# First Fourier factor, direct S5 products and angle tables in another order, the tables in smaller pieces

## The chip, the cores and the metric

One core of a Trainium2 chip runs the whole kernel. The metric is the time of one execution on the device, in microseconds (us). Of several executions the median is given.

## What is computed

The kernel computes two layers of a trunk over 2048 latent tokens (a grid of width 64) and 256 context tokens, 1024 channels wide, in fp32. The first layer has two branches side by side: a Fourier mixer and a windowed attention. The second layer's branches are a gated MLP and a bidirectional linear recurrence (S5). Cut to the lines that matter:

```python
def even_mixer(hl, hc, w_in, ...):
    fa_l, ga_l, q_l, k_l, v_l, gb_l = split_cols(hl @ w_in, EVEN_SPLITS)
    a_l = fourier_mix(fa_l) * jax.nn.silu(ga_l)
    n_l = neighbourhood_attention(heads(q_l), heads(k_l), heads(v_l), k_c, v_c, rpb) * jax.nn.silu(gb_l)
    y_l = jnp.concatenate([a_l, n_l], axis=-1) @ w_out

def fourier_mix(v):
    y = jnp.fft.fftn(vg, axes=(1, 3), norm="ortho").real

def s5_discretise(lam_re, lam_im, log_step, b_re, b_im):
    dt = jnp.exp(log_step)[:, None]
    lam_bar = jnp.exp(lam * dt)
    b_bar = ((lam_bar - 1.0) / lam)[..., None] * lax.complex(b_re, b_im)

def s5_direction(u_lat, u_ctx, ...):
    h_lat = linear_scan(lam_bar, drive(u_lat), h_end, reverse)
    return read(h_lat)
```

The 2048-point transform over positions is done as two factors (16 times 128). The recurrence's tables depend on weights alone and are made during the first layer.

## The kernel before

The program of the first layer stands in `run`. The normalised input is kept on the chip as two fp16 halves, hh and hl, and a weight as wh and wl; an fp32 product is three fp16 passes into one PSUM tile pg (`mm3`, L181). In this order, the program does:

- `fourier_proj`: the Fourier branch's projection; its rows go to memory as fa_d.
- `s5_prep` (L1116): the recurrence's tables. It ends in two parts. The direct products (L1298 to L1330) load ws and bs from memory for each of eight q, multiply them (matmuls of L1319), mask and add on DVE (L1329) and store kp_d. The angle tables (L1332 to L1340) are complex products of two "turn" tables by `cmul` (L1109 to L1114, six DVE operations); each of eight pieces (four j, two directions d) is a tile rot of 128x2304, stored to rot_d by SP (L1340). The pool of the turn tables, s5r, lies on the left side of memory and is closed behind them.
- `v_proj` (L528): the values in three blocks of 256 columns, 18 tiles of 128 tokens each. Blocks 0 and 1 are called from within `s5_prep`, block 2 after it.
- `fourier_first` (L548): for each of 16 n2 it loads a factor d and the transposed rows Z of fa_d (L559, L561), multiplies (L564), copies on ScalarE (ACT) and stores A_d (L567); then come the context's part (L573, L577) and its output ys (L581). d and Z have three buffers each.
- `heads` (L686): for each of six pairs of heads the weights, then ten tiles of Q and K (drained into stg, stored as qd and kd, L739 and L741) and five gate tiles (drained into gate, L526). It is a generator of steps: `need((0, 5))` runs all steps of pair 0, and the attention takes the later ones as filler.
- `attention` (L817): the pool "units", on the right side. The loads (masks L883, K L911, Vc L917, G L920, Q L905, V L931) are issued on SP. For each unit a score tile S (L997, one buffer) is followed by the softmax on DVE (L1000, into P) and ACT (L1002), transposes PT (L1016), their split into halves, and the value product pv (L1030, L1033).

All loads and stores of this stretch go through SP's one queue, in program order. The compiler's scheduler decides each engine's order by its own estimates; inside the attention PE's order is that of the code, where `fill` puts QK and gate tiles of the coming pairs between scores. Every engine runs its own list in order, and a wait at its head holds all that follow.

Much later, in the second layer, the tables are read back as E (L1650): one piece (j, d) is read in two halves h, four runs of 1152 B for each partition and half.

Of the kernel before, what the change touches and what calls it, by code (L numbers as in the profile page):

```python
# [9 lines left out]
F32 = mybir.dt.float32  # L10
# [44 lines left out]
class Kern:  # L55
# [137 lines left out]
    def run(self):  # L193
        with ExitStack() as st:
# [13 lines left out]
            with self.pool_("ps0", space=PSUM) as self.ps:  # L208
# [4 lines left out]
                with self.pool_("gemm", side="right") as gp:  # L213
# [334 lines left out]
    def fourier_first(self, pool):  # L548
# [7 lines left out]
        self.gg_d = self.dram.tile([2, 128, SEQ], F32, name="gg_d")  # L556
        for n2 in range(16):
# [558 lines left out]
    def s5_prep(self, between):  # L1116
# [7 lines left out]
        self.rot_d = self.dram.tile([4, 2, 128, 2 * 4 * 288], F32, name="rot_d")  # L1124
        self.mag8 = self.const.tile([128, 32], F32, name="mag8")
        rots = ExitStack()
        rp = rots.enter_context(self.pool_("s5r"))

        turn = [rp.tile([128, 2, 32, n], F32, name=f"turn{n}") for n in (16, 18)]
# [166 lines left out]

        with self.stream(""):
            between[1]()  # L1298
        with self.pool_("s5pk") as pool:
# [571 lines left out]
```

## Time and profile before

| | before |
|---|---|
| median of 3 runs | 2426.11 us (2421.2 to 2430.19) |
| the profiled execution's own time | 2425.14 us |
| its span in the trace | 2423.3 us |
| mean granted clock of PE | 0.965 |
| PE busy | 2219.7 us (92%) |
| DVE busy | 1579.7 us (65%) |
| ACT busy | 1050.9 us (43%) |
| DMA, mean rate | 141 GB/s |

The span runs from the first to the last instruction of the trace; the 1.8 us by which the execution's own time is longer lie around it. Busy shares are averages over stages with different limits, so the stage in question is read by windows and timelines. A timeline row gives the start and duration of a group of like instructions, and in brackets the idle time before it and what ended it. [...]

### The profile page before, as it was taken

Reading aid. Unit: us, or ns where it says so; the run is one execution under the profiler, and the core shown is the slowest. Engines: PE = TensorE matmul, PEld = TensorE weight load, DVE = VectorE, ACT = ScalarE, POOL = GpSimd, SP = SyncE. Lnnn points to the kernel's source line nnn. Section 1 sums busy time; section 2 is a strip of 40 time slices with the busy share of each in tenths; the row PEclk is TensorE's granted clock in tenths of the full one; section 3 lists DMA queues with packets and bytes.
Section 4 is the critical chain, followed back from the end, with each engine's and each line's share of the span. In section 5 each row is a group of like instructions: output and inputs, shape, how many; then the busy total and the mean of one; then the engine's idle time right before and its main releaser. Section 6 shows DMA issues by size and latency. Waiting matters only on the chain. (4 is left out here: it accounts for less than half of the span.)

```text
span 2423.3 us, 42852 instructions
## 1 busy us (share of the span) xinstructions
PE 2219.7 (92%) x15860; PEld 1421.6 (59%) x15860; DVE 1579.7 (65%) x3949; ACT 1050.9 (43%) x2212; POOL 336.3 (14%) x457
## 2 busy tenths in 40 slices
PE   5999885999999999999978899997899999999998
PEld 2668773476665767666657466556555565444443
DVE  5888892266567666666569667774496952458455
ACT  4822222155555656565557454552221221334332
POOL 0102200022222322222234000000010011110000
PEclk8999998999999999999998899998899999999999
DMA  9844677413335243433342444545466751256332
GB/s 320 264 108 127 168 236 231 131 54 95 115 103 149 81 119 106 116 114 93 96 167 86 137 140 135 158 134 164 143 182 195 200 152 48 80 156 194 122 113 87
DMA packets 349971, 340.57 MB, mean 141 GB/s; under 512 B 94482, under 2 KB 291486, under 8 KB 347970
## 3 DMA queue, kind: packets, MB, share of 16 engines
q1 hardware_dynamic: 349650, 337.80, 46.5%
q8 instruction: 125, 2.05, 0.4%
q14 instruction: 84, 0.69, 0.1%
q10 hardware_dynamic: 112, 0.03, 0.0%
HBM read 218.43 MB, written 110.91 MB: 136 GB/s over the span
## 5 line engine op out<-in xcount | busy, mean ns | idle before, releaser
L181 PEld LDWEIGHTS <-wh 128*128 128x128 f16 x2944 | 281.8, 99 | 169.0 <-issue 9.2
L1000 DVE CUSTOM_DVE_ANT_0 P<-S,bias,slab 128x640 f32<-128x640 f32 (+2 forms) x216 | 193.6, 896 | 161.0 <-PE S L997 157.0
L189 ACT ACTIVATE ph<-PT 128x384 f16<-128x384 f32 (+1 forms) x408 | 172.6, 456 | 216.4 <-PE PT L1016 215.6
L181 PEld LDWEIGHTS <-wl 128*128 128x128 f16 x1472 | 144.0, 100 | 112.0 <-issue 27.4
L190 DVE SCALAR_TENSOR_TENSOR pl<-PT,ph 128x384 f16<-128x384 f32 (+1 forms) x408 | 195.0, 508 | 13.8 <-ACT ph L189 12.4
L949 POOL TENSOR_TENSOR bias<-G,masks 128x384 f32<-128x384 f32 (+1 forms) x144 | 152.3, 1058 | 345.5 <-DVE t L1000 322.5
L1002 ACT ACTIVATE P<-P,t 128x640 f32<-128x640 f32 (+2 forms) x216 | 181.2, 839 | 41.4 <-DVE t L1000 40.0
L181 PE MATMUL pg<-hh,wl 128*128 128x512 f16 (+1 forms) x800 | 184.6, 365 | 13.7 <-DVE stg L190 5.6
L181 PEld LDWEIGHTS <-h1p 128*128 128x128 f16 x1152 | 111.1, 98 | 136.6 <-issue 8.8
L181 PE MATMUL pu<-wh,h1p 128*128 128x512 f16 x768 | 179.9, 379 | 1.6 <-DMA h1p<-h 1.6
L181 PE MATMUL pg<-hl,wh 128*128 128x512 f16 (+1 forms) x800 | 181.2, 360 | 0.0
L181 PE MATMUL pg<-hh,wh 128*128 128x512 f16 (+1 forms) x800 | 181.2, 359 | 0.0
L181 PEld LDWEIGHTS <-yh 128*128 128x128 f16 x1088 | 106.8, 98 | 125.4 <-issue 2.7
L1016 PE MATMUL PT<-ident,P 128*128 128x128 f32 x1104 | 162.3, 277 | 11.3 <-DVE pl L190 9.8
L997 PEld LDWEIGHTS <-Q 128*128 128x128 f16 x1776 | 131.6, 98 | 63.1 <-issue 22.7
L997 PE MATMUL S<-K,Q 128*128 128x128 f16 (+1 forms) x1776 | 158.4, 233 | 2.4 <-DVE t L1000 2.2
L181 PE MATMUL pg<-wh,yl 128*128 128x512 f16 x544 | 133.3, 386 | 5.2 <-DVE yl L190 5.1
L1016 PEld LDWEIGHTS PT<-ident,P 128*128 128x128 f32 x1104 | 120.3, 142 | 20.2 <-issue 6.8
L181 PE MATMUL pg<-wl,yh 128*128 128x512 f16 x544 | 131.3, 382 | 0.0
L156 DVE TENSOR_REDUCE t<-wf 128x1 f32<-128x1024 f32 x68 | 82.4, 1216 | 74.8 <-DMA wf<-in_w_in_even_dram 27.0
L181 PE MATMUL pg<-wh,yh 128*128 128x512 f16 x544 | 130.3, 379 | 0.0
L181 PEld LDWEIGHTS <-hh 128*128 128x128 f16 x1152 | 115.5, 100 | 15.7
(344 smaller groups left out, 3952.6 us busy)
## 6 DMA issues: line engine op xcount, KB each, us to landing
wada<-in_w_ada_dram SPq DMA_DIRECT2D x34, 512.0 KB
x<-in_x_dram SPq DMA_DIRECT2D x32, 512.0 KB
wf<-in_w_in_even_dram SPq DMA_DIRECT2D x28, 512.0 KB
V<-vs SPq DMA_DIRECT2D x192, 64.0 KB
K<-kd SPq DMA_DIRECT2D x96, 128.0 KB
wf<-in_w_in_odd_dram SPq DMA_DIRECT2D x20, 512.0 KB
rot_d<-rot SPq DMA_DIRECT2D x8, 1152.0 KB
Y<-ys SPq DMA_DIRECT2D x144, 64.0 KB
```

What stands on the lines that cost most here:

```text
L156: nc.vector.tensor_reduce(m[:, i:i + 1], f, axis=AX.X, op=OP.max, apply_absolute_value=True)
L181: nc.tensor.matmul(ps, a(k), b(k), start=(n == 0), stop=(n == 3 * kb - 1))
L189: nc.scalar.activation(hi, src, AF.Copy, scale=scale)
L190: nc.vector.scalar_tensor_tensor(lo, src, scale, hi, op0=OP.mult, op1=OP.subtract)
L949: nc.gpsimd.tensor_tensor(q4(bv), gv, q4(masks[:, m0:m0 + 128 * nch]), op=OP.add)
L997: nc.tensor.matmul(S[:, at:at + m], u["q"], K[:, hl, off:off + m], start=(hl == 1), stop=(hl == 0))
L1000: nc.vector.tensor_tensor_reduce(P[:, 0:n], S[:, 0:n], u["B"][:, 0:n], u["negf"], 3.4e38, OP.add, OP.min, nm)
L1002: nc.scalar.activation(P[:, 0:n], P[:, 0:n], AF.Exp, bias=nm, scale=-1.0, accum_out=l)
L1016: self.nc.tensor.transpose(PT[:, c - a:c - a + 128], P[:, c:c + 128], self.ident)
```

## The change

`s5_prep` is cut into three. Its first part, with value blocks 0 and 1, stays where it is. The direct products become `s5_direct`, which loads ws and bs for two j at a time and no longer for four. The angle tables become `s5_angles`: sixteen pieces of half the size, in the layout in which E is read back. The turn tables' pool goes to the right side of memory and stays open to the end.

`fourier_first` becomes a generator that issues its first four pairs of loads and then yields. The new order of the program is: tables of S5, value blocks 0 and 1; weights of pair 0; the Fourier factor's first loads; value block 2; the rest of the Fourier factor; the direct products; all steps of pair 0; the angle tables, in a pool of their own on the right side; the attention.

```diff
-                    with self.stream("b"):
-                        self.s5_prep([lambda: self.v_proj(gp, 0), lambda: self.v_proj(gp, 1)])
-                    self.v_proj(gp, 2)
-                    qp = hTs.enter_context(self.pool_("qkg"))
-                    with self.pool_("fft") as fp, self.stream("f"):
-                        self.fourier_first(fp)
-                    self.gpool = hTs.enter_context(self.pool_("gates"))
-                    self.steps = self.mixed(self.heads(qp), self.ada_steps(), ADA_EVERY)
-                    self.ahead, self.credit, self.at, self.made = None, 0.0, (0, 0), -1
-                    self.need((0, 5))
+                    with self.pool_("s5r", side="right") as rp:
+                        with self.stream("b"):
+                            self.s5_prep(rp, [lambda: self.v_proj(gp, 0), lambda: self.v_proj(gp, 1)])
+                        qp = hTs.enter_context(self.pool_("qkg"))
+                        self.steps = self.mixed(self.heads(qp), self.ada_steps(), ADA_EVERY)
+                        self.ahead, self.credit, self.at, self.made = None, 0.0, (0, 0), -1
+                        while self.ahead is None:
+                            self.step()
+                        with self.pool_("fft") as fp:
+                            first = self.fourier_first(fp)
+                            next(first)
+                            self.v_proj(gp, 2)
+                            with self.stream("f"):
+                                for _ in first:
+                                    pass
+                            with self.stream("b"):
+                                self.s5_direct()
+                        self.gpool = hTs.enter_context(self.pool_("gates"))
+                        self.need((0, 5))
+                        with self.pool_("s5e", side="right") as pool:
+                            self.s5_angles(pool)
...
+        for _ in range(4):
+            load()
+        yield
         for n2 in range(16):
-            dt = pool.tile([128, 2, 128], F32, name=self.name("d1"), tag="d1", bufs=3)
-            nc.sync.dma_start(dt, I["k_dft1"][:, n2])
-            Z = pool.tile([128, 256], F32, name=self.name("Z"), tag="Z", bufs=3)
-            nc.sync.dma_start(Z, dap(self.fa_d, n2 * 256, [[16 * 256, 128], [1, 256]]))
+            dt, Z = got[n2]
...
+            if n2 < 12:
+                load()
...
+    def s5_direct(self):
...
             for q in range(8):
-                ws = pool.tile([128, 4, 2, 144], F32, name=self.name("ws"), tag="ws", bufs=2)
...
+                for j4 in range(4):
+                    j = j4 % 2
+                    if j == 0:
+                        g = 4 * q + j4
+                        ws = pool.tile([128, 2, 2, 144], F32, name=self.name("ws"), tag="ws", bufs=2)
+                        bs = pool.tile([128, 2, 2, 16], F32, name=self.name("bs"), tag="bs", bufs=2)
...
-            tp = [t([128, 4, 18, 16]) for _ in range(2)]
-            for j in range(4):
-                for d in range(2):
-                    e = pool.tile([128, 2, 4, 288], F32, name=self.name("rot"), tag="rot", bufs=2)
...
-                    self.bq.dma_start(self.rot_d[j, d], e.rearrange("p r g n -> p (r g n)"))
-        rots.close()
+    def s5_angles(self, pool):
...
+        tp = [pool.tile([128, 2, 18, 16], F32, name=self.name("tq"), tag=f"tq{k}") for k in range(2)]
+        for i in range(16):
+            j, h, d = i // 4, i // 2 % 2, i % 2
+            e = pool.tile([128, 2, 2, 288], F32, name=self.name("rot"), tag="rot", bufs=2)
...
+            self.cmul(nc.vector, [e[:, r].rearrange("p g (b k) -> p g b k", k=16) for r in range(2)], x, y, tp)
+            nc.sync.dma_start(self.rot_d[j, h, d], e.rearrange("p r g n -> p (r g n)"))
...
-            nc.sync.dma_start(e, dap(self.rot_d, (j * 2 + d) * 128 * 2304 + 2 * h * 288,
-                                     [[2304, 128], [1152, 2], [288, 2], [1, 288]]))
+            nc.sync.dma_start(e.rearrange("p r g n -> p (r g n)"), self.rot_d[j, h, d])
```

What this does to the engines' lists is seen at three places. Line numbers of the changed program are its own; a number behind a name is the buffer's.

SP before, at the end of the Fourier part and the start of the attention (A_d and ys are Fourier stores, wf a weight, the rest the attention's loads):

```order
L581 DMA ys_118<-yc_4701 128x256
L581 DMA ys_119<-yc_4713 128x256
L883 DMA masks<-in_k_mask_dram 128x3840
L917 DMA Vc_5334<-vs_126 128x256 x2
L920 DMA G_5337<-gd_1751 128x768
L920 DMA G_5338<-gd_1752 128x768
L931 DMA V_5359<-vs_126 128x256 x2
L154 DMA wf_5097<-in_w_in_even_dram 128x8x128
L931 DMA V_5359<-vs_126 128x256 x2
L154 DMA wf_5155<-in_w_in_even_dram 128x8x128
L931 DMA V_5364<-vs_126 128x256 x4
```

SP in the changed program, at the same loads:

```order
L1373 DMA rot_d<-rot_5198 128x1152
L1373 DMA rot_d<-rot_5206 128x1152
L906 DMA masks<-in_k_mask_dram 128x3840
L934 DMA K_5428<-kd_4756 64x2x256 x2
L934 DMA K_5431<-kd_4756 64x2x256 x2
L940 DMA Vc_5434<-vs_126 128x256 x2
L943 DMA G_5437<-gd_1751 128x768
L943 DMA G_5438<-gd_1752 128x768
L934 DMA K_5443<-kd_4756 64x2x512 x2
L934 DMA K_5446<-kd_4756 64x2x512 x2
L934 DMA K_5449<-kd_4756 64x2x512 x2
```

Before, masks, Vc and G stand right behind the Fourier stores, and the V loads and then K and Q between weights and stores. Now all of them stand in one block behind the sixteenth and last table write; fourteen table writes with no qd or kd store between them precede it.

DVE before, between the weights of pair 0 (wl) and its first QK tiles (stg):

```order
L190 SCALAR_TENSOR_TENSOR wl_4778<-wf_4746,slab_217,wh_4777 128x1024
L190 SCALAR_TENSOR_TENSOR wl_5113<-wf_5033,slab_217,wh_5112 128x1024
L921 TENSOR_SCALAR G_5337<-G_5337,slab_217 128x768
L921 TENSOR_SCALAR G_5338<-G_5338,slab_217 128x768
L190 SCALAR_TENSOR_TENSOR stg_4817<-pg_4792,stg_4817 128x256
L156 TENSOR_REDUCE t_5096<-wf_5097 128x1
L156 TENSOR_REDUCE t_5154<-wf_5155 128x1
L190 SCALAR_TENSOR_TENSOR stg_4847<-pg_4822,stg_4847 128x256
L190 SCALAR_TENSOR_TENSOR stg_4877<-pg_4852,stg_4877 128x512
L190 SCALAR_TENSOR_TENSOR stg_4907<-pg_4882,stg_4907 128x512
```

DVE in the changed program, at the last gate tiles of pair 0 (gate), and then where the tables end and the attention begins (P is the first softmax):

```order
L537 SCALAR_TENSOR_TENSOR gate_5360<-th_5386,pg_5361 128x512
L1135 TENSOR_TENSOR tq_5084<-turn_1855,turn_1854 128x576
L1136 TENSOR_TENSOR tq_5085<-turn_1855,turn_1854 128x576
L537 SCALAR_TENSOR_TENSOR gate_5390<-th_5416,pg_5391 128x256
L1137 TENSOR_TENSOR rot_5134<-tq_5084,tq_5085 128x576
L1132 TENSOR_TENSOR tq_5084<-turn_1855,turn_1854 128x576
L1133 TENSOR_TENSOR tq_5085<-turn_1855,turn_1854 128x576
L1134 TENSOR_TENSOR rot_5142<-tq_5084,tq_5085 128x576
```

```order
L1134 TENSOR_TENSOR rot_5206<-tq_5084,tq_5085 128x576
L1135 TENSOR_TENSOR tq_5084<-turn_1855,turn_1854 128x576
L1136 TENSOR_TENSOR tq_5085<-turn_1855,turn_1854 128x576
L1137 TENSOR_TENSOR rot_5206<-tq_5084,tq_5085 128x576
L944 TENSOR_SCALAR G_5437<-G_5437,slab_217 128x768
L944 TENSOR_SCALAR G_5438<-G_5438,slab_217 128x768
L1023 ISA P_5485,t_5486<-S_5476,bias_5424,slab_217 128x640
L1023 ISA t_5486 128x1
```

Before, the tables are over long before this place. Now 41 of the 96 table operations stand between the seventh QK tile's drain (stg_4962) and the last gate (gate_5390), among QK and gate drains and the weights of the next pair, and 55 in a row between that gate and G.

PE before, where the first score tile ends (pg_5125 is a gate tile of pair 0):

```order
L997 MATMUL S_5376<-K_5349,Q_5355 128x128
L997 LDWEIGHTS Q_5355
L997 MATMUL S_5376<-K_5349,Q_5355 128x128
L181 LDWEIGHTS wl_4778
L181 MATMUL pg_5125<-hh_74,wl_4778 128x512
L181 LDWEIGHTS wl_4778
L181 MATMUL pg_5125<-hh_74,wl_4778 128x512
```

PE in the changed program, where the first score tile begins (pg_5391 is the last gate tile of pair 0):

```order
L181 LDWEIGHTS wh_3689
L181 MATMUL pg_5391<-hh_78,wh_3689 128x256
L1020 LDWEIGHTS Q_5455
L1020 MATMUL S_5476<-K_5428,Q_5455 128x256
L1020 LDWEIGHTS Q_5455
L1020 MATMUL S_5476<-K_5428,Q_5455 128x256
L1020 LDWEIGHTS Q_5455
L1020 MATMUL S_5476<-K_5443,Q_5455 128x128
```

Before, gate tiles of 512 columns stand between the first score tiles. Now all gate tiles of pair 0 stand ahead of the first score, and the five score tiles S_5476, S_5493, S_5510, S_5540 and S_5584 have only two transposes and one value product between them; then comes the first QK tile of pair 1, pg_5602 (pg_5502 before). From there on PE, DVE, ACT and POOL have the same order in both programs.

## Rows read from the trace of the kernel before

**Rows 1.** Windows: us, busy (x count) PE, PEld, DVE, ACT, POOL; PEclk, DMA share, GB/s.

```profile
292.70:357.80 65.10, 62.56 (x688) 55.65 (x688) 58.70 (x87) 18.19 (x51) 0.00 (x0) 1.00 0.77 236
357.80:373.90 16.10, 0.00 (x0) 0.00 (x0) 8.40 (x8) 0.33 (x1) 0.00 (x0) 0.66 0.65 233
373.90:410.30 36.40, 25.30 (x81) 16.28 (x82) 0.84 (x2) 10.93 (x18) 0.00 (x0) 0.92 0.65 220
...
415.40:470.30 54.90, 51.14 (x240) 25.21 (x241) 15.57 (x18) 6.66 (x11) 1.82 (x2) 0.92 0.62 169
470.30:498.50 28.20, 28.20 (x186) 16.49 (x185) 16.26 (x47) 14.30 (x26) 3.06 (x4) 1.00 0.23 66
498.50:600.00 101.50, 100.42 (x950) 71.30 (x948) 65.38 (x168) 59.38 (x139) 27.43 (x43) 1.00 0.26 71
```

**Rows 2.** PE timeline: start us, us, group xcount [idle before <-releaser].

```profile
293.41 1.83 PE L1319 MATMUL pg<-ws,bs 128*16 128x112 f32 x32 [0.71 <-DMA bs<-bst_d]
...
373.98 6.63 PE L564 MATMUL pg<-Z,d 128*128 128x256 f32 x16 [16.27 <-DMA Z<-fa_d]
...
383.77 1.10 PE L564 MATMUL pg<-Z,d 128*128 128x256 f32 x4 [1.30 <-DMA Z<-fa_d]
...
415.39 1.89 PE L181 MATMUL pg<-hh,wl 128*128 128x256 f16 x8 [3.94 <-DVE slab L717]
...
463.44 1.89 PE L181 MATMUL pg<-hh,wh 128*128 128x512 f16 x8
...
470.35 0.72 PE L997 MATMUL S<-K,Q 128*128 128x256 f16 x8
...
498.48 0.60 PE L181 MATMUL pg<-hh,wl 128*128 128x256 f16 x4
```

**Rows 3.** DVE lines by form, 160 to 500 us: busy us, mean ns | idle before.

```profile
L190 DVE SCALAR_TENSOR_TENSOR wl<-wf,slab,wh 128x1024 f16<-128x1024 f32 x12 | 16.0, 1347 | 0.6 <-ACT wh L189 0.6
...
L1109 DVE TENSOR_TENSOR p<-turn,turn 128x1152 f32<-128x1152 f32 x8 | 10.9, 1357 | 0.2
...
L1277 DVE TENSOR_TENSOR W<-p,p 128x576 f32<-128x576 f32 x8 | 6.6, 850 | 0.1
...
L190 DVE SCALAR_TENSOR_TENSOR stg<-pg,stg 128x512 f16<-128x512 f32 x8 | 5.5, 689 | 23.7 <-ACT stg L189 23.7
...
L1000 DVE CUSTOM_DVE_ANT_0 P<-S,bias,slab 128x640 f32<-128x640 f32 x5 | 4.4, 882 | 5.2 <-PE S L997 5.0
```

**Rows 4.** DVE timeline, 253 to 257 us: operations of the S5 weights, 128x576.

```profile
253.87 0.75 DVE L1276 TENSOR_TENSOR p<-p,p 128x576 f32<-128x576 f32 x1
254.66 1.43 DVE L1277 TENSOR_TENSOR W<-p,p 128x576 f32<-128x576 f32 x2
256.00 0.75 DVE L1278 TENSOR_TENSOR p<-p,p 128x576 f32<-128x576 f32 x1
256.67 0.75 DVE L1279 TENSOR_TENSOR p<-p,p 128x576 f32<-128x576 f32 x1
```

**Rows 5.** SP queue timeline, 366 to 452 us: start us, issue us, transfer xcount.

```profile
366.33 0.32 SPq L1340 DMA_DIRECT2D rot_d<-rot  x1
...
379.85 0.49 SPq L561 DMA_DIRECT2D Z<-fa_d  x1
...
411.48 0.33 SPq L883 DMA_DIRECT2D masks<-in_k_mask_dram  x1
...
412.82 0.93 SPq L920 DMA_DIRECT2D G<-gd  x2
...
418.94 4.93 SPq L931 DMA_DIRECT2D V<-vs  x7
...
442.79 2.50 SPq L911 DMA_DIRECT2D K<-kd  x4
...
451.76 0.80 SPq L905 DMA_DIRECT2D Q<-qd  x2
```

**Rows 6.** What L1667 (ACT, second layer) waited for: us, times.

```profile
  DMA E<-rot_d: 0.7, 1
```

More of the change, by code (lines that the diff above doesn't have):

```diff
@@ L556, in fourier_first, with load @@
         self.gg_d = self.dram.tile([2, 128, SEQ], F32, name="gg_d")
+        got = []
+        def load():
+            n2 = len(got)
+            dt = pool.tile([128, 2, 128], F32, name=self.name("d1"), tag="d1", bufs=4)
+            nc.sync.dma_start(dt, I["k_dft1"][:, n2])
+            Z = pool.tile([128, 256], F32, name=self.name("Z"), tag="Z", bufs=4)
+            nc.sync.dma_start(Z, dap(self.fa_d, n2 * 256, [[16 * 256, 128], [1, 256]]))
+            got.append((dt, Z))
+        for _ in range(4):
+            load()
+        yield
         for n2 in range(16):
-            dt = pool.tile([128, 2, 128], F32, name=self.name("d1"), tag="d1", bufs=3)
-            nc.sync.dma_start(dt, I["k_dft1"][:, n2])
-            Z = pool.tile([128, 256], F32, name=self.name("Z"), tag="Z", bufs=3)
-            nc.sync.dma_start(Z, dap(self.fa_d, n2 * 256, [[16 * 256, 128], [1, 256]]))
+            dt, Z = got[n2]
             ps = self.psg()
@@ L1114, in cmul, with s5_prep @@
         eng.tensor_tensor(o[1], t[0], t[1], op=OP.add)
-    def s5_prep(self, between):
+    def s5_prep(self, rp, between):
         nc, I, tc = self.nc, self.I, self.tc
@@ L1123, in s5_prep @@
         bst_d = self.dram.tile([32 * 4 * 64, 16], F32, name="bst_d")
-        self.rot_d = self.dram.tile([4, 2, 128, 2 * 4 * 288], F32, name="rot_d")
+        self.rot_d = self.dram.tile([4, 2, 2, 128, 2 * 2 * 288], F32, name="rot_d")
         self.mag8 = self.const.tile([128, 32], F32, name="mag8")
-        rots = ExitStack()
-        rp = rots.enter_context(self.pool_("s5r"))
-        turn = [rp.tile([128, 2, 32, n], F32, name=f"turn{n}") for n in (16, 18)]
+        self.turn_t = turn = [rp.tile([128, 2, 32, n], F32, name=f"turn{n}") for n in (16, 18)]
         with self.pool_("s5p") as pool, ExitStack() as early:
@@ L1295, in s5_prep @@
                         self.bq.dma_start(self.min_d[g0 + gp], m)
+        self.bst_d = bst_d
         with self.stream(""):
             between[1]()
+    def s5_direct(self):
+        nc, I = self.nc, self.I
+        bst_d = self.bst_d
         with self.pool_("s5pk") as pool:
@@ L1311, in s5_prep @@
             for q in range(8):
[L1312 to L1315 removed]
                 ps = self.psg((128, 240))
[L1317 to L1318 removed]
+                for j4 in range(4):
[4 more added lines that the diff above has]
+                        bs = pool.tile([128, 2, 2, 16], F32, name=self.name("bs"), tag="bs", bufs=2)
+                        self.bq.dma_start(ws, dap(self.mo_d, g * 256 * 144, [[144, 128], [128 * 144, 4], [1, 144]]))
+                        self.bq.dma_start(bs, dap(bst_d, g * 256 * 16, [[16, 128], [128 * 16, 4], [1, 16]]))
+                    o = ps[32 * j4:32 * j4 + 16]
                     f = lambda out, d, c0, n, st, sp: nc.tensor.matmul(out, bs[:, j, d], ws[:, j, d, c0:c0 + n], start=st,
@@ L1330, in s5_prep @@
                 self.bq.dma_start(self.kp_d[q], kp)
-            tp = [t([128, 4, 18, 16]) for _ in range(2)]
-            for j in range(4):
-                for d in range(2):
-                    e = pool.tile([128, 2, 4, 288], F32, name=self.name("rot"), tag="rot", bufs=2)
-                    q = slice(16 * d + 4 * j, 16 * d + 4 * j + 4)
-                    x = [turn[1][:, r, q, :, None].to_broadcast([128, 4, 18, 16]) for r in range(2)]
-                    y = [turn[0][:, r, q, None, :].to_broadcast([128, 4, 18, 16]) for r in range(2)]
-                    self.cmul(nc.vector, [e[:, r].rearrange("p g (b k) -> p g b k", k=16) for r in range(2)], x, y, tp)
-                    self.bq.dma_start(self.rot_d[j, d], e.rearrange("p r g n -> p (r g n)"))
-        rots.close()
+    def s5_angles(self, pool):
+        nc = self.nc
+        turn = self.turn_t
+        tp = [pool.tile([128, 2, 18, 16], F32, name=self.name("tq"), tag=f"tq{k}") for k in range(2)]
+        for i in range(16):
+            j, h, d = i // 4, i // 2 % 2, i % 2
+            e = pool.tile([128, 2, 2, 288], F32, name=self.name("rot"), tag="rot", bufs=2)
+            q = slice(16 * d + 2 * (i // 2), 16 * d + 2 * (i // 2) + 2)
+            x = [turn[1][:, r, q, :, None].to_broadcast([128, 2, 18, 16]) for r in range(2)]
+            y = [turn[0][:, r, q, None, :].to_broadcast([128, 2, 18, 16]) for r in range(2)]
+            self.cmul(nc.vector, [e[:, r].rearrange("p g (b k) -> p g b k", k=16) for r in range(2)], x, y, tp)
+            nc.sync.dma_start(self.rot_d[j, h, d], e.rearrange("p r g n -> p (r g n)"))
     def out_proj(self, pool, lh, ll, w, u_y, ssq, sx, sq=None):
```

4 lines of the change are left out of this document (removed).

## The prediction, before the changed kernel ran

> **What bounds the kernel now.** I read the busy shares first, then the windows by stage, then the timelines of PE, DVE and SP around the moved work. TensorE (PE) is the busiest engine, so what the change is worth is read from PE's idle time there [rows 1]. The reader is to see three things there. From 292.7 to 357.8 us, where value block 2 runs beside the direct products, PE is busy 62.56 of 65.10 us. From 357.8 to 415.4 it is nearly empty: nothing at all in 16.10 us and 25.30 of the next 36.40, and the PE timeline names the waits [rows 2]: 16.27 us for Z, the transposed Fourier input that is read back from memory, a few more waits for Z after that, then 3.94 for DVE's constants of pair 0. From 470.3 on PE is full (28.20 of 28.20, 100.42 of 101.50). So some 35 us are there to be won between 357.8 and 470.3, and any delay at the end of the stretch is handed on in full, because nothing behind it has slack. VectorE (DVE) does 48 table operations of 1.357 us before 366.3 [rows 3], under value block 2, where PE is the bound and they cost PE nothing; 8.40 us of the empty 16.10 are table work.
>
> The orders give the point at which both programs stand alike: the first matmul of pair 1's first QK tile (pg_5502 before, pg_5602 after). Ahead of it both have done five score tiles, two transposes and one value product; behind it the engines do the same things in the same order. Before reaches it at 498.48 us [rows 2]. The forecast is the time at which the changed kernel reaches it.
>
> **PE up to the first table operation.** Value block 1 ends at about 292.7; the direct product of q 0 now stands ahead of its last five tiles (1.83 us [rows 2]), so take 294.5. Behind it PE does, now mixed:
> - value block 2: the window's 62.56 us less eight direct products of 1.83 is 47.9 (2.66 a tile, 18 tiles);
> - the first Fourier factor and the context's: 25.30 us at a granted clock of 0.92, so 23.3 at full clock [rows 1];
> - seven direct products, 12.8;
> - seven QK tiles: two of 256 columns (2.66 each) and five of 512. 463.44 to 470.35 is 32 matmuls, so 24 take 5.18 [rows 2]: together 31.2.
>
> That is 115.2, and 409.7. The waits for Z are meant to lie under value tiles now. The direct products bring waits of their own: their first one before waited 0.71 us for bs, and the loads come in half the size and twice the number, one pair ahead, on the same SP queue. I bound the stalls by nothing and by 14 us (the waits in the 36.40 us window and the 3.94, together, cost 15) and take 5. With 1.3 us for ACT and DVE to drain the seventh tile, the tables start at **416**.
>
> **DVE through the tables.** 96 operations of 128x576 take the place of 48 of 128x1152. Four operations of this size stand in a row in [rows 4]: 0.67 us from start to start where the next does not need the last, 0.79 where it does. A piece has six, three of them dependent: 0.73 each, 70 us in all (before: 48 at 1.357, 65). [rows 3] has a slow form of the size at 0.85, which bounds it from above at 82; 0.67 throughout bounds it from below at 64. [...]
>
> Among the tables DVE also does three stg of 0.69, three wl of 1.35, four and a half gates like stg, two reductions near a wl in size and some 25 constants: 14 us. So the last table is written at 416 + 70 + 14 = **500**. PE has by then long finished: three more QK tiles and four and a half gate tiles are 39 us, so it stops near 457, and 55 table operations in a row (40 us) stand on DVE between the last gate and the first score's softmax. This is the place that decides: nothing is left for PE to do meanwhile.
>
> **SP and the loads behind the tables.** Before, masks, Vc and G were issued at 411 to 413, and V, K and Q from then on, between the stores that feed them [rows 5]; at 470.35 the first scores found all of it there. In the changed order every one of these loads stands behind the last table write, in one queue. From there to the second Q: masks 0.33, two K for the context and four for bands 0 and 1 with two halves each (12 issues of 0.62, 7.5 us), Vc and G 1.9, Q 0.4 each: 10.5 us. A load is used some 3.9 us after its issue (Z at 379.85, PE at 383.77 [rows 2, 5]); I take 3.5 behind the last issue. So the first scores start at 500 + 14 = **514**. Below 13 it cannot be by these rows. Above: up to the Q these are 3.4 MB, 14.7 us at the 233 GB/s of the busiest stretches here [rows 1], and the V behind them go on for 12 issues of up to 0.70, so I bound it at 18.
>
> **The start of attention without filler.** Before, each score tile was followed by 5.2 us of gate tiles, so softmax cost PE nothing. Now S_5476, S_5493, S_5510, S_5540 and S_5584 have only two transposes and one value product between them. The score tile has one buffer, so each waits for DVE's 0.88 us on the one before: four times 0.72 + 0.88 and a last 0.72 [rows 2, 3], 7.1, with the value product waiting for the last V, 8.5. Bounds 7 (all of that hidden) and 12 (PE at the lower of its two levels after so long a pause; the first group after the 16.27 us wait took 6.63 us for 16 matmuls that later took 1.10 for four [rows 2]).
>
> **Sum.** 514 + 8.5 = 522.5 against 498.5: **+24 us**. The profiled execution took 2425.1 us, 1.0 below the median of 2426.1, so the forecast is **2449**. The bounds together: all low, 293 + 115.2 + 0.7 + 64 + 12 + 13 + 7 = 505, +6; all high, 294.5 + 115.2 + 14 + 1.5 + 82 + 15 + 18 + 12 = 552, +54.
>
> **Costed at nothing.** Reading the tables back as one run of 4608 B instead of four of 1152: before, one use waited 0.7 us for E [rows 6], so at most that is gained. The turn tables' memory is held longer on the right side; the orders show no load pushed back by it before the tables. The Fourier stores and direct-product stores are now mixed on SP; what they could hold up is in the 5 us of stalls.
>
> **Rivals.**
> - **Faster: the mixing pays and the tables hold nobody.** It needs the last table before about 475 for break-even (475 + 14 + 8.5 = 498), and before 440 for the whole gain: then PE wins back its 35 us, 2390. For it: the 35 us are real and the waits for Z do go. [...] Against it: DVE would have to start the tables 25 us before PE has produced the seventh tile, and 115 us of PE work stand ahead of that. Chance 0.09.
> - **About even.** No stalls and quick operations: 5 us less stalling, 6 less for operations at 0.67 and 1 elsewhere leave +12 or a little less, 2436. For it: the waits for the direct loads have a whole value tile each to hide in. Chance 0.16.
> - **Slower still: the table writes hold DVE.** rot has two buffers; a write (590 KB) has 4.4 us of the next piece and 1.5 of the one after, 5.9 us, before its buffer is wanted. If it takes 7.4, each of 14 pieces waits 1.5: +21 on top, 2470. A landing of 3.9 us speaks against it, the busy DMA engines (0.62 to 0.77 of their time [rows 1]) for it. Chance 0.11.
>
> The forecast itself keeps 0.64. About 0.5%, 12 us, is what a measurement of this kernel can tell from no change. Only the first rival lies below it on the fast side (0.09); the even case lies within it (0.16); the forecast and the third rival lie above it (0.75). The range, **2430 to 2470**, leaves out the first rival, half of the third and a little of the even case. It is narrower than the bounds together since they would all have to fall on one side.
>
> **What would show it.** In the changed profile: no wait of 16 us for Z; value tiles, Fourier tiles and direct products mixed, and over before 400; the first L1132 of 128x576 near 416, its last near 500, with 55 in a row; masks issued right behind the last rot_d; PE idle for some 55 us up to the first S near 514; pg_5602 near 522. The prediction is wrong if the first scores start before 490, if the pause of PE is under 30 us, or if the span from that point to the end is not the 1925 us it was before.

## The result, and the profile after

The changed kernel takes 2446.83 us (median of 5 runs, 2440.05 to 2451.45) against 2424.17 us: the ratio is 1.0083, 95% interval 1.0068 to 1.0099. It is slower, by 22.7 us where 24 were forecast, and at 2446.83 where 2449 was named. The profiled execution has a span of 2445.0 us (2423.3 before) and a mean granted clock of 0.959 (1.00 is full speed).

Windows of the changed kernel, columns as in [rows 1]:

```profile
292.70:357.80 65.10, 61.41 (x465) 51.21 (x466) 16.27 (x34) 19.01 (x37) 0.00 (x0) 0.95 0.68 204
357.80:412.70 54.90, 54.90 (x450) 35.88 (x449) 11.58 (x39) 14.64 (x36) 0.31 (x1) 1.00 0.46 112
412.70:451.00 38.30, 38.30 (x193) 18.89 (x190) 37.67 (x77) 9.82 (x13) 0.00 (x0) 1.00 0.44 149
451.00:511.00 60.00, 0.02 (x2) 0.02 (x2) 44.85 (x63) 1.59 (x3) 2.12 (x3) 0.53 0.50 167
511.00:522.20 11.20, 7.75 (x61) 6.22 (x62) 5.62 (x16) 5.61 (x13) 1.82 (x2) 0.61 0.56 159
522.20:625.00 102.80, 101.73 (x968) 72.47 (x966) 67.17 (x174) 60.09 (x142) 28.63 (x45) 1.00 0.30 83
```

PE's timeline of the changed kernel, the rows that answer to [rows 2] (L1020 is the score's line now, L1023 the softmax's):

```profile
295.28 0.80 PE L109 MATMUL mx<-ident,t 128*128 128x128 f32 x2 [4.36 <-DMA bs<-bst_d]
...
510.99 1.25 PE L1020 MATMUL S<-K,Q 128*128 128x256 f16 x8 [59.98 <-DMA Q<-qd]
513.33 1.23 PE L1020 MATMUL S<-K,Q 128*128 128x256 f16 x8 [1.10 <-DVE t L1023]
...
521.64 0.72 PE L1020 MATMUL S<-K,Q 128*128 128x256 f16 x8
522.19 0.60 PE L181 MATMUL pg<-hh,wl 128*128 128x256 f16 x4
```

From 357.8 to 451 us PE is busy throughout, 54.90 of 54.90 us and 38.30 of 38.30, where before it had two windows nearly empty [rows 1]. All of pair 0's gate tiles are done at 451. Then it stands still for 59.98 us, and the first four of the five score tiles that follow take 1.23 to 1.25 us for their eight matmuls (0.72 before), at a granted clock of 0.61 in that stretch. The point at which both programs stand alike, pg_5602, is reached at 522.19 in place of 498.48, which is 23.7 us later. The span is only 21.7 us longer, so behind that point the changed kernel is 2 us quicker. What PE waits for is read from DVE and SP. DVE of the changed kernel:

```profile
411.43 0.17 DVE L1358 TENSOR_TENSOR p<-p,p 16x16 f32<-16x16 f32 x1 [0.22 <-ACT p L1357]
412.13 0.69 DVE L190 SCALAR_TENSOR_TENSOR stg<-pg,stg 128x512 f16<-128x512 f32 x1 [0.53 <-ACT stg L189]
412.73 0.75 DVE L1132 TENSOR_TENSOR tq<-turn,turn 128x576 f32<-128x576 f32 x1
...
454.21 0.41 DVE L537 SCALAR_TENSOR_TENSOR gate<-th,pg 128x256 f32<-128x256 f32 x1
...
455.32 0.76 DVE L1132 TENSOR_TENSOR tq<-turn,turn 128x576 f32<-128x576 f32 x1
...
459.83 0.76 DVE L1132 TENSOR_TENSOR tq<-turn,turn 128x576 f32<-128x576 f32 x1
...
494.31 0.75 DVE L1136 TENSOR_TENSOR tq<-turn,turn 128x576 f32<-128x576 f32 x1
495.09 0.76 DVE L1137 TENSOR_TENSOR rot<-tq,tq 128x576 f32<-128x576 f32 x1
504.70 0.62 DVE L944 TENSOR_SCALAR G<-G,slab 128x768 f32<-128x768 f32 x1 [8.85 <-DMA G<-gd]
```

The direct products' last addition is at 411.43 (L1358), the seventh QK tile's drain at 412.13, and the first table operation right behind it, at 412.73. The last gate is drained at 454.21; the last table operation starts at 495.09 and ends at 495.85. Then DVE has nothing to do for 8.85 us, because G has not come. SP of the changed kernel (start, issue time, transfer xcount):

```profile
455.32 40.88 SPq L1373 DMA_DIRECT2D rot_d<-rot  x10
496.25 0.42 SPq L906 DMA_DIRECT2D masks<-in_k_mask_dram  x1
496.73 2.87 SPq L934 DMA_DIRECT2D K<-kd  x4
...
502.67 5.04 SPq L934 DMA_DIRECT2D K<-kd  x8
507.75 1.06 SPq L928 DMA_DIRECT2D Q<-qd  x2
508.85 5.66 SPq L954 DMA_DIRECT2D V<-vs  x12
```

Masks leave 0.4 us behind the last table operation, right behind the last table write; K and Q come behind them; the second Q's issue ends at 508.8 and the scores start at 510.99.

### The profile page after: what moved, and what is told of

It reads as the page before. It is cut to its first block, busy times and chain, and to the rows that moved or that the text cites. A ratio compares the mean times of both kernels' runs of the same rounds, so it can differ in the third digit from the quotient of the medians.

```text
span 2445.0 us, 42934 instructions
## 1 busy us (share of the span) xinstructions
PE 2211.3 (90%) x15860; PEld 1419.1 (58%) x15860; DVE 1585.9 (65%) x3997; ACT 1050.8 (43%) x2212; POOL 336.1 (14%) x457
## 5 line engine op out<-in xcount | busy, mean ns | idle before, releaser
L1023 DVE CUSTOM_DVE_ANT_0 P<-S,bias,slab 128x640 f32<-128x640 f32 (+2 forms) x216 | 193.6, 896 | 164.7 <-PE S L1020 161.0
L1020 PE MATMUL S<-K,Q 128*128 128x128 f16 (+1 forms) x1776 | 162.3, 236 | 64.8 <-DMA Q<-qd 60.0
L1020 PEld LDWEIGHTS <-Q 128*128 128x128 f16 x1776 | 133.8, 100 | 126.2 <-DMA Q<-qd 60.3
L190 DVE SCALAR_TENSOR_TENSOR pl<-PT,ph 128x384 f16<-128x384 f32 (+1 forms) x408 | 195.1, 508 | 14.3 <-ACT ph L189 12.9
```

Source lines behind the costliest of these rows:

```text
L190: nc.vector.scalar_tensor_tensor(lo, src, scale, hi, op0=OP.mult, op1=OP.subtract)
L1020: nc.tensor.matmul(S[:, at:at + m], u["q"], K[:, hl, off:off + m], start=(hl == 1), stop=(hl == 0))
L1023: nc.vector.tensor_tensor_reduce(P[:, 0:n], S[:, 0:n], u["B"][:, 0:n], u["negf"], 3.4e38, OP.add, OP.min, nm)
```

## The experiments

Every run was made beside runs of the kernel before on the same chip, whose medians were 2424 to 2429 us; each ratio is to those, so runs are best compared by their ratios. "Point" is the start of the tile that answers to pg_5602, "tables" are the start of the first table operation and the end of the last.

| run | tables, us | masks issued | first score | point | median, us | ratio (95%) |
|---|---|---|---|---|---|---|
| before | 283.8 to 366.3 | 411.48 | 470.35 | 498.48 | 2424.17 | 1 |
| changed | 412.7 to 495.9 | 496.25 | 510.99 | 522.19 | 2446.83 | 1.0083 (1.0068 to 1.0099) |
| e1 | one piece, 408.6 to 413.1 | 442.65 | 459.05 | 471.45 | 2395.83 | 0.9872 (0.9857 to 0.9888) |
| e2 | 283.4 to 379.8 | 446.57 | 461.61 | 475.15 | 2401.64 | 0.9894 (0.9876 to 0.9912) |
| e3 | 380.6 to 474.2 | 474.60 | 490.12 | 501.32 | 2426.71 | 1.0000 (0.9991 to 1.0010) |
| e4 | 377.9 to 472.8 | 473.20 | 488.64 | 501.04 | 2421.26 | 0.9976 (0.9966 to 0.9986) |
| e5 | 282.0 to 378.2 | 442.66 | 458.24 | 472.26 | 2399.55 | 0.9879 (0.9863 to 0.9895) |
| e6 | 286.3 to 379.2 | | 482.55 | 510.69 | 2438.85 | 1.0033 (1.0020 to 1.0046) |
| e7 | 413.4 to 497.3 | 468.49 | 510.61 | 521.81 | 2445.13 | 1.0066 (1.0049 to 1.0083) |
| e8 | 282.8 to 378.8 | 460.34 | 475.81 | 489.57 | 2420.80 | 0.9961 (0.9945 to 0.9978) |
| e9 | 415.5 to 503.7 | 504.13 | 520.21 | 531.42 | 2457.50 | 1.0124 (1.0106 to 1.0142) |
| e10 | one piece, to 294 | 411.37 | 470.46 | 498.60 | 2425.43 | 0.9992 (0.9980 to 1.0004) |
| e11 | 282.7 to 399.9 | 423.30 | 468.63 | 496.76 | 2421.99 | 0.9968 (0.9955 to 0.9980) |

From the point to the end of the span it is 1920 to 1928 us in all of them but e8 (1934.6), so the point tells nearly the whole story of each.

**e1: the tables' computation taken away, their writes kept.**

```diff
-            e = pool.tile([128, 2, 2, 288], F32, ...)
+            if i == 0:
+                e = pool.tile([128, 2, 2, 288], F32, ...)
...
-            self.cmul(...)
+            if i == 0:
+                self.cmul(...)
```

> The changed kernel with the first table piece computed once and stored sixteen times: 90 of the 96 table operations are left out, all table writes and the whole order around them stay. Theory A (the last table operation and the loads behind its write set the end): the first scores no longer wait for DVE; they start when the gate tiles end, near 452 to 460 us in place of 511, pg_5602 near 460 to 470, and the time is 2385 to 2400. Theory B (the mixed order of values, Fourier factor and direct products costs by itself): still above 2424, since nothing of the mix is undone. Theory C (the writes and the loads behind them in SP's queue hold the attention, not DVE): most of the loss stays, 2430 to 2447, since all sixteen writes are still there.

2395.83 us: theory A's range (the point is 1.5 us beyond it), and B and C fall. PE's pause shrinks from 59.98 to 12.13 us:

```profile
459.05 1.25 PE L1020 MATMUL S<-K,Q 128*128 128x256 f16 x8 [12.13 <-DMA Q<-qd]
```

What is left is SP's. Its queue holds the sixteen table writes between 413 and 435, among stores of Q and K, then weight loads, two more stores and only then the masks:

```profile
427.83 7.42 SPq L1375 DMA_DIRECT2D rot_d<-rot  x6
...
442.65 0.43 SPq L906 DMA_DIRECT2D masks<-in_k_mask_dram  x1
```

The scores come 16.4 us behind the masks. The mixed front stayed whole; with hardly any table work left the kernel is 1.28%, some 31 us, faster than before. That the front is worth this much with all the table work in it is for e2 and e5 to show.

**e2: the tables early again.** Their call is moved ahead of value block 2, in the same pool on the right side; three buffers for d and Z and two for a make room.

```diff
                             next(first)
+                            with self.pool_("s5e", side="right") as pool:
+                                self.s5_angles(pool)
                             self.v_proj(gp, 2)
...
                         self.need((0, 5))
-                        with self.pool_("s5e", side="right") as pool:
-                            self.s5_angles(pool)
```

> The changed kernel with the angle tables (half pieces, right side) made ahead of value block 2 in place of last; to make room the Fourier factor's buffers go from 4 to 3 and 3 to 2. Theory A: tables lie under value block 2 and the Fourier factor (some 72 us of PE work against 70 us of tables and 6 us of value drains on DVE), the attention's loads go out between the QK stores, scores stand between gate tiles again: 2383 to 2400, faster than both kernels. Theory B (the mix costs): 2424 or more. Theory D (the half-sized pieces cost, wherever they stand): at least 5 us above what A says, since 96 small ones take 70 us against 65 for 48 large ones.

2401.64 us, 1.06% faster than before, though 2 us above what A allowed. Whether D (the small pieces) costs those 2 us can't be told from the other waits that the trace names: PE waits 6.53 us for a value drain of block 1 and 4.31 for a weight scale, both behind tables on DVE, and some 5 for direct products.

**e5: the same with the tables' call behind value block 2.**

```diff
                             next(first)
-                            with self.pool_("s5e", side="right") as pool:
-                                self.s5_angles(pool)
                             self.v_proj(gp, 2)
+                            with self.pool_("s5e", side="right") as pool:
+                                self.s5_angles(pool)
```

> As e2_early, but the tables stand behind value block 2 in the program, so that the value drains go ahead of them on DVE. In e2_early the tables began at 283 us among block 1's last drains and PE waited 6.5 us for a drain, 4.3 for a weight scale and 4.3 for direct products. Theory A: with the drains first these waits shrink, and the point pg_5602 comes at 462 to 472 (475.15 in e2_early): 2388 to 2400. If the tables' place in the program makes no difference to DVE's order among the drains: 2400 to 2404, as e2_early.

2399.55 us, 1.21% faster than before; with e2, whose interval overlaps, it is the fastest kernel here that does all the work. The time is at the end of A's range and the point 0.3 us beyond it, and the reason given was wrong: the tables still begin at 282.0 and the waits are still there. Rows of PE's timeline:

```profile
289.40 1.87 PE L181 MATMUL pg<-wh,hl 128*128 128x256 f16 x8 [7.18 <-DVE v L190]
...
304.07 1.07 PE L181 MATMUL pg<-wh,hl 128*128 128x256 f16 x8 [3.89 <-ACT wh L189]
...
458.24 0.73 PE L1020 MATMUL S<-K,Q 128*128 128x256 f16 x8 [0.73 <-DMA Q<-qd]
```

By its ratio e5 can't be told from e1, which has hardly any tables but a pause of 12.13 us ahead of its scores; what the early tables still cost is not shown. Why the early tables begin at 282 to 283 wherever their call stands, DVE's row tells:

```profile
281.99 0.76 DVE L1132 TENSOR_TENSOR tq<-turn,turn 128x576 f32<-128x576 f32 x1 [2.60 <-DMA min_d<-mi]
```

The first table operation waits 2.60 us for the store of mi, a tile of the S5 weights that it does not read (likewise in e2, e8 and e11, 1.8 to 2.6 us). What e4 leads to, below, fits this.

**e3: the tables last, the rest of the program in the order of before.** `s5_direct` is called behind `s5_prep`, then come value block 2, the whole Fourier factor, and pair 0.

```diff
                             self.s5_prep(rp, [lambda: self.v_proj(gp, 0), lambda: self.v_proj(gp, 1)])
+                            self.s5_direct()
+                        self.v_proj(gp, 2)
                         qp = hTs.enter_context(self.pool_("qkg"))
...
+                        with self.pool_("fft") as fp, self.stream("f"):
+                            for _ in self.fourier_first(fp):
+                                pass
...
                         self.need((0, 5))
                         with self.pool_("s5e", side="right") as pool:
```

> The tables last, in half pieces on the right side, but the Fourier factor, value block 2, direct products and weights of pair 0 in the order of the kernel before. Theory A: the mix's gain is hidden behind the tables, so undoing it changes little: DVE starts the tables near 405 at the end of the Fourier factor, needs some 85 to 88 us for them and the drains, last table near 492, scores 14 later, pg_5602 near 515, time 2438 to 2452. If gain and loss simply add (Theory E: the mix gains its 35 to 40 us of PE wherever the tables stand, the late tables cost 60): near 2485. Theory B (the mix costs): near 2424.

2426.71 us, no different from before, and 20 us quicker than the changed kernel. A missed by 11 us and E (2485) by far. B's number (near 2424) was met, but by luck: e1 had refuted its reason, and the mix was not undone here, as is seen below, so e3 does not test it. As for A, the tables began at 380.6, not 405, so the last one was written at 474.2 and not 492. The steps behind it are those of A (masks at once, scores 15.5 us later, the point 11.2 after that). And the program's order did not unmix anything: with the tables away, the scheduler put the Fourier products between the value tiles itself (groups of six in PE's timeline from 350 to 367 us). The wait for Z was gone.

**e4: the tables' pool on the left side, one word changed.**

```diff
-                        with self.pool_("s5e", side="right") as pool:
+                        with self.pool_("s5e") as pool:
```

> The changed kernel with the tables' pool on the left side of memory, nothing else. Theory A: only the start of the tables moves, since the place they get is free some ten DVE steps earlier; 19 instead of 55 table operations stand behind the last gate; last table near 470 to 475, scores 14 later, pg_5602 near 493 to 498, time 2417 to 2426. If the side of memory itself (waits of the attention's tiles for the tables' place) were the loss, all of it would go: below 2400. If the side does not matter: 2447.

2421.26 us: A's number, 25 us below the changed kernel, and the third expectation (no effect) falls. The last table at 472.75 is in A's range too, the point at 501.04 is 3 us beyond it. But A had the size from the order of the operations, and the trace tells what makes it. DVE of e3 and of e4, the last work of the Fourier factor (yc) and the first table operation:

```profile
377.76 0.42 DVE L596 TENSOR_TENSOR yc<-pg,gga 128x256 f32<-128x256 f32 x1 [2.74 <-PE pg L594]
...
380.62 0.75 DVE L1126 TENSOR_TENSOR tq<-turn,turn 128x576 f32<-128x576 f32 x1
```

```profile
377.09 0.42 DVE L602 TENSOR_TENSOR yc<-pg,gga 128x256 f32<-128x256 f32 x1
377.89 0.75 DVE L1132 TENSOR_TENSOR tq<-turn,turn 128x576 f32<-128x576 f32 x1
```

The tables begin within 3 us of the Fourier factor's last product with its gate, and in the changed kernel within 1.3 us of the last direct product. So theory F: they begin when the last user of their place in memory is done. In the changed kernel itself the first table operation waits for nothing; it stands on DVE's list right behind the drain at 412.13. That the direct products are what holds the place there is inferred from the times.

**e9: only the direct products put back to their old place.**

```diff
                             self.s5_prep(rp, [lambda: self.v_proj(gp, 0), lambda: self.v_proj(gp, 1)])
+                            self.s5_direct()
...
-                            with self.stream("b"):
-                                self.s5_direct()
```

> The changed kernel with the direct products alone put back to their old place behind the S5 weights; the tables stay last, on the right side. Theory F (new: the tables' place in memory is the direct products' and the Fourier factor's; that is why they begin at 413 in the changed kernel, and at 381 to 383 in e3 and e4): the tables begin near 381, their last write comes near 474 to 478, scores 15 later, pg_5602 near 501 to 505: 2424 to 2431. If the start of the tables is set by DVE's place in the order or by the Fourier factor and the weights being mixed into value block 2, not by the direct products: they still begin after 400 and the time is 2438 to 2447.

2457.50 us, above both ranges. The tables began at 415.5: after 400, as the second expectation has it, and not near 381, as F's has it. The rows show who used the place last:

```profile
414.66 0.42 DVE L601 TENSOR_TENSOR yc<-pg,gga 128x256 f32<-128x256 f32 x1 [0.35 <-PE pg L599]
415.45 0.75 DVE L1131 TENSOR_TENSOR tq<-turn,turn 128x576 f32<-128x576 f32 x1
417.94 0.76 DVE L1132 TENSOR_TENSOR tq<-turn,turn 128x576 f32<-128x576 f32 x1 [1.74 <-DMA ys<-yc]
```

Again they begin right behind the Fourier factor's last product, and their second operation waits for the store of it. It is the Fourier factor that came 37 us later than in e3. In e9 the direct products stand alone on PE, without value tiles between them; PE waits 0.2 to 6 us before most of them, mainly for bs, and then 11.12 us for the scales of value block 2's weights. So F fits the changed kernel, e3, e4 and e9, here after the fact: the expectation had the wrong last user, and that the direct products held the place in the changed kernel is not shown. That the side of the pool sets the start is shown by e4, with nothing else changed; that table operations wait for stores which do not concern them, by the 1.74 us here and the 2.60 in e5.

**e7: the table writes issued by ACT.**

```diff
-            nc.sync.dma_start(self.rot_d[j, h, d], ...)
+            nc.scalar.dma_start(self.rot_d[j, h, d], ...)
```

> The changed kernel with the table writes issued by ACT in place of SP; nothing else. If SP's order alone holds the attention's loads (the prediction's words: they stand behind the last table write in one queue), masks goes out near 450 and the loads lie under the tables; the scores then wait for DVE only, near 497, and the time falls by 12 to 14 us to 2432 to 2436. If the loads are held a second time, because their tiles lie where the tables' tiles lay, the first K load still leaves after the last table operation at 496 and the time stays at 2444 to 2449.

2445.13 us: the second expectation. SP of e7:

```profile
468.49 0.34 SPq L906 DMA_DIRECT2D masks<-in_k_mask_dram  x1
497.26 2.86 SPq L934 DMA_DIRECT2D K<-kd  x4
```

With the writes out of that queue, masks left 28 us ahead of the tables' end, but the first K only with it, at 497.26. The one queue that the prediction spoke of is real, but taking the writes out of it gains nothing here: something else holds the loads until the tables are done as well. The trace names it (SP's waits from 400 to 520 us: total, times, longest):

```profile
SPq L934 <- DVE rot L1137: 21.8, 1, 21.8
...
SPq L906 <- DMA rot_d<-rot: 15.0, 1, 15.0
...
SPq L934 <- DMA rot_d<-rot: 6.6, 1, 6.6
```

The masks wait for a table write on the other queue, and the first K for a table write and then for a table operation on DVE. Neither load reads a table, so what is left is the memory in which the tables lie. No run frees both at once (the left side and ACT's queue together).

**e6: the kernel before with half pieces, in the new layout.**

```diff
-                    e = pool.tile([128, 2, 4, 288], F32, ...)
+                    e = pool.tile([128, 2, 2, 288], F32, ...)
...
-                    self.bq.dma_start(self.rot_d[j, d], ...)
+                    self.bq.dma_start(self.rot_d[j, h, d], ...)
```

> The kernel before with one thing changed: sixteen tables of half the size, stored in the new layout and read back in one run, at the old place. Theory A: DVE has 5 us more to do under value block 2, where PE is the bound, and the last pieces run into the wait for Z, which they do not end: within 3 us of before (2424 to 2431). Theory D (the small pieces cost on the path): 5 us or more slower, 2432 or above. If the contiguous read of E is worth something: 2 us or more faster.

The ratio is 1.0033 (1.0020 to 1.0046), some 8 us slower; in the profiled executions the point is 12.2 us later. A falls and D stands: the last table operation and PE's wait for Z in e6 are

```profile
378.44 0.76 DVE L1114 TENSOR_TENSOR rot<-p,p 128x576 f32<-128x576 f32 x1
```

```profile
385.54 6.67 PE L564 MATMUL pg<-Z,d 128*128 128x256 f32 x16 [25.92 <-DMA Z<-fa_d]
```

The tables end 12.9 us later than before and PE starts on Z 11.6 us later (385.54, 373.98 before [rows 2]). So in the kernel before, too, the tables set the time: Z's loads stood behind the last table write.

**e10: the kernel before with one table piece computed.**

```diff
-                    e = pool.tile([128, 2, 4, 288], F32, ...)
+                    if j == d == 0:
+                        e = pool.tile([128, 2, 4, 288], F32, ...)
...
-                    self.cmul(nc.vector, ...)
+                    if j == d == 0:
+                        self.cmul(nc.vector, ...)
```

> The kernel before with the first of its eight table pieces computed once and stored eight times: 42 of 48 table operations are left out. Theory F, for the kernel before: its wait of 16.27 us for Z was the tables' (Z is issued on SP behind the last table write, into memory that the tables' pools held), so without them the Fourier factor moves under value block 2 and the wait goes: no wait for Z above 3 us, the point pg_5502 near 463 to 472 in place of 498.48, time 2388 to 2400. If the wait for Z is that of the transposed read itself (the prediction read it so): it stays above 10 us and the time is within 6 us of before.

The long wait for Z is gone (the longest left is 2.56 us), as F says; the time is not lower, though by F it should be. PE's timeline of e10:

```profile
322.64 3.06 PE L1319 MATMUL pg<-ws,bs 128*16 128x112 f32 x32 [7.58 <-DMA bs<-bst_d]
...
333.92 3.20 PE L1319 MATMUL pg<-ws,bs 128*16 128x112 f32 x32 [8.21 <-DMA bs<-bst_d]
...
383.72 1.10 PE L564 MATMUL pg<-Z,d 128*128 128x256 f32 x4 [1.09 <-DMA Z<-fa_d]
...
387.39 2.04 PE L564 MATMUL pg<-Z,d 128*128 128x256 f32 x4 [2.56 <-DMA Z<-fa_d]
```

SP's queue in e10:

```profile
301.88 5.62 SPq L1342 DMA_DIRECT2D rot_d<-rot  x5
307.60 1.15 SPq L1314 DMA_DIRECT2D ws<-mo_d  x1
308.79 8.78 SPq L1315 DMA_DIRECT2D bs<-bst_d  x1
317.61 2.72 SPq L1342 DMA_DIRECT2D rot_d<-rot  x1
```

Eight writes of 1152 KB left from 302 to 323 us. A bs load behind the first five of them needed 8.78 us for its issue alone (0.53 to 1.58 in the kernel before), and PE waited 7.58 and 8.21 us for bs, together 15.8, where it had waited 16.27 for Z. So e6 and e10 together show that the wait for Z was the tables'; what the tables cost the kernel before in all is not shown.

**e8: the tables ahead of pair 0's weights, full Fourier buffers.**

```diff
+                        with self.pool_("s5e", side="right") as pool:
+                            self.s5_angles(pool)
                         qp = hTs.enter_context(self.pool_("qkg"))
...
-                        with self.pool_("s5e", side="right") as pool:
-                            self.s5_angles(pool)
```

> The changed kernel with the tables in a pool of their own ahead of pair 0's weights, the Fourier buffers as in the change. The Fourier factor's tiles then lie partly where the tables lay, so its loads stand behind the table writes on SP. Theory A: tables off the end, but the Fourier factor comes late and is no longer spread over value block 2; it is mixed with QK tiles instead, which are as good a filler, so the point comes near 465 to 480: 2390 to 2408. If the gain of the mix hangs on the Fourier factor being under value block 2: above 2410.

2420.80 us, above A's range, as the second expectation has it. The Fourier factor ran at 383 to 433 us, mixed with the direct products and QK tiles. PE waited 7.23 and 2.18 us for value drains and 6.70 for a weight half between 283 and 315, more than in e5, and 2.04, 1.13, 2.00, 1.75 and 3.70 us for bs of the last direct products, which stood with little between them, between 437 and 455. Which of these the place of the Fourier factor is to blame for stays open.

**e11: e2 with the direct products at their old place.**

```diff
                             self.s5_prep(rp, [lambda: self.v_proj(gp, 0), lambda: self.v_proj(gp, 1)])
+                            self.s5_direct()
...
-                            with self.stream("b"):
-                                self.s5_direct()
```

> Tables early and on the right side as in e2_early (under value block 2, half pieces, Fourier buffers 3 and 2), and the direct products at their old place ahead of them, so that they stop neither the tables nor the QK tiles. Theory A and F together: no wait for Z, no wait for direct products among the QK tiles (4 to 5 us in e2 and e5), scores between gate tiles: point at 462 to 470, time 2386 to 2397, the fastest of all. If the tables' delay of the value drains (7 us in e2 and e5) is what keeps those at 2400: 2397 to 2403.

2421.99 us, neither expectation. PE's timeline of e11:

```profile
323.64 3.29 PE L1347 MATMUL pg<-ws,bs 128*16 128x112 f32 x32 [1.97 <-DMA bs<-bst_d]
...
346.27 0.80 PE L109 MATMUL mx<-ident,t 128*128 128x128 f32 x2 [13.80 <-DVE t L161]
```

As in e9, the direct products alone on PE wait for bs (ten waits of 0.8 to 3 us), and 13.80 us more for the scales of value block 2.

## Why the prediction was right, and where it was not

The sum, against the trace:

| step | forecast | measured |
|---|---|---|
| first table operation | 416 | 412.73 |
| last table written | 500 | 495.85 |
| first score | 514 | 510.99 |
| pg_5602 | 522.5 | 522.19 |

- **PE up to the tables.** 115.2 us of work and 5 of stalls were near: the front had one large stall, 4.36 us for bs, and small ones. The waits for Z went, as said. The mix was to be over before 400 and was not: the last direct products ran on PE from 408.00, and their last addition at 411.43 is what stands just ahead of the tables.
- **DVE through the tables.** 84 us forecast, 83.1 measured (412.73 to 495.85); pieces in the row of 55 are 4.51 us apart (L1132 at 455.32 and 459.83), 0.75 an operation where 0.73 was taken. Four of the six operations wait for the one ahead of them and not three: two read its result, and two write a tile tq that it has just read. So the tables' own 70 us were some 72, and the drains and weights among them some 11 in place of 14. What the halving itself costs, e6 shows: 96 table operations of 128x576 are busy for some 72 us there (0.750 to 0.758 each) and before 48 of 128x1152 for 64.9 (1.348 to 1.359 each). That is some 7 of the 12.9 us by which e6's tables end later.
- **Loads.** 14 us forecast, 15.1 measured; over the kernels with the tables last, masks to score is 14.7 to 16.1 (e7, where masks left early, apart).
- **Scores without filler.** 8.5 us forecast, 11.2 measured, inside the bound of 12. This term was undersized: four of the five score tiles ran at a lower clock (1.23 to 1.25 us, the granted clock of the stretch 0.61), which the forecast had put into the bound and not into the value. These 2.7 us and 1.1 in the loads made up for the 3.3 us by which the tables began early and 0.9 in DVE's term, so that the point was hit within 0.3 us by luck; each term alone was within 3.3. The two levels of which the forecast spoke are 0.50 and 1.00 in the traces: in the changed kernel 0.50 from 511 to 518 us and 1.00 from 520 on; in the kernel before, behind the wait of 16.27 us, 0.50 from 374 to 378 and 1.00 from 380 to 410.3.
- **Behind the point** the span is 1922.8 us, 1924.8 before: handed on, as said.

Two statements that the sum did not need were wrong:

- "They cost PE nothing" (the 48 table operations under value block 2). e6 moved their end by 12.9 us and the wait for Z by 11.6; e10 took them away and that wait went, though other waits came in its place and the time stayed. The 8.40 us of table work in the empty window were there to be read [rows 1], and so was the order on SP: the last table write left at 366.33 [rows 5] and the first Z behind it, at 369.38.
- "The orders show no load pushed back by it before the tables." The place in memory of the tables decides when they start: with the pool on the other side (e4) they start 35 us earlier and the loss is gone. The prediction took DVE's order as given; what had made it, by theory F the last use of that place, it did not ask. The expectation of e3, which reasoned in the same way, was 11 us off.

Of the rivals, the first named the prize: with the tables off the end (e1, e2, e5) the time is 2396 to 2402, where 2390 was given; its condition, a last table before about 475, was met by e3 and e4 (474.2, 472.8), which came out even, as its sum has it. Mixing pays here on a condition: the mixed front is worth 1.1 to 1.3% in e1, e2 and e5, and the kernel loses 0.83% while a row of 55 operations stands behind it. The third rival did not occur: table operations follow each other without a wait for a write.

Not tried: the attention's loads ahead of late tables; late tables on the left side with their writes on ACT; and which part of e10's burst of writes delays which load.

## What to carry to other kernels

Work that is moved last must be followed to the engine that ends it, and from there through the queue and the memory behind it: here 83 us of DVE work, then 15 us of loads, then 11 us of a start without filler, in a row, and PE idle for 60 us of them. A pool's side is part of the schedule: in e4 it alone moved the start of the work by 35 us, and in e7 the loads waited for the tables although the tables' writes were on another queue. And before calling a stretch hidden, look at what is queued behind its last instruction.

## What the runs showed of the hardware

- After the pause of 59.98 us the granted clock was 0.61 between 511.0 and 522.2, and eight score matmuls took 1.25 us in place of 0.72; from 521.64 on they took 0.72 again. After the pause of 12.13 us in e1 all five score tiles, from 459.05 to 470.40, took 1.23 to 1.25 us, and the next one, at 475.34, took 0.72; the granted clock was 0.78 between 460 and 490.
- In the changed kernel's row of 55 table operations, fp32 of 128x576 on DVE, each took 0.75 to 0.76 us; they started 0.67 to 0.68 us apart where independent, 0.79 where one reads what the last one wrote or writes over what it read (455.32 to 459.83 us). With four of six waiting in this way, a table piece took 4.51 us.
- Behind five table writes of 1152 KB issued in a row (e10, 301.9 to 307.5 us) a small load's issue took 8.78 us on SP's queue, against 0.53 to 1.58 in the kernel before, and PE waited 7.6 and 8.2 us for bs, where the kernel before waited 0.7 at most.
